# Smaller weight buffers, a fixed order of products: an edit to the GEMM pipeline of a two-layer decoder trunk

## The chip, the cores and the metric

The kernel runs on one core of one Trainium2 chip. The metric is the device time of one execution in microseconds (us), the median of several runs. Each core has five engines with a queue each: TensorE (PE; its weight loader is shown as PEld), VectorE (DVE), ScalarE (ACT), GpSimd (POOL) and SyncE (SP). DMA transfers are issued from the queues of SP and ACT and carried by 16 DMA engines. PE reads weights and activations from on-chip memory (SBUF) and adds up its products in PSUM.

## The reference: what is computed

A decoder trunk of two layers over 272 tokens (16 learned meta tokens and 256 of the sequence), width 2048, 16 heads of 128, in float32. Layer 0 uses attention with forget gates, layer 1 stick-breaking attention over a K/V that is projected once. Each layer ends with a squared-ReLU MLP of inner width 8192. Cut to what matters:

```python
a = rms_norm(h, norm_attn[0])
q, k, v, f_logit = split(a @ fox_w_in[0])            # 2048 -> 3*2048 + 16
o = forgetting_attention(q, k, v, cumsum(log_sigmoid(f_logit + fox_b_f[0])))
h = h + o @ fox_w_o[0]
h = h + squared_relu_mlp(rms_norm(h, norm_mlp[0]), w_up[0], w_down[0])
a, c = rms_norm(h, norm_attn[1]), rms_norm(h, kv_norm)
o = stick_breaking_attention(a @ sb_w_q[0], *split(c @ w_kv))
h = h + o @ sb_w_o[0]
h = h + squared_relu_mlp(rms_norm(h, norm_mlp[1]), w_up[1], w_down[1])
return rms_norm(h, final_norm)[:, 16:]               # without the meta tokens
```

## The kernel before

**Layout.** Everything is feature-major: activations are tiles of 128 features by 272 tokens, 16 such chunks for the width of 2048 (`hT`, the residual stream). In layer 1, where the output needs only the 256 sequence tokens, most products have 256 columns.

**Split numbers.** PE multiplies operands of type F32R. To keep float32 accuracy, each operand is split into a high part, which is the F32R copy made by ACT, and a low part, which is what DVE finds left over. A product of weight and activation is then three products on PE: high x high (line 220), high x low (221) and low x high (222). In layer 1 the groups are "paired" (`pairs`): the high and low activations lie side by side, 512 columns wide, so line 217 multiplies both with the high weights in one product, and line 218 multiplies the high activations with the low weights (256 columns). Splits of the weights are made on the chip as they are read: `whi` (line 197, ACT) and `wlo` (line 198, DVE), two chunks of 512 columns (a half) at a time.

**A GEMM group** (`gemm_group`, line 161) makes 512 output features, in four accumulators of 128 features (`accs`, index `m`), from 2048 input features. It takes its weights in four quarters (`kb`) of four input chunks (`kc`) each. For each quarter it loads 1 MB of weights into one raw buffer (`raw`, pool `wraw`, three buffers, line 185, issued from SP), splits it as two halves (`hf`, pool `wspl`, three buffers each for `whi` and `wlo`), and then writes down the products. The order of the products (lines 203 to 207) is: in quarters 0 to 2, first half before second half, and in each half output chunk by output chunk; in the last quarter output chunk by output chunk through all four input chunks, so that the accumulators are finished one after another. After the last product of an output chunk its evacuation (`evac`) is written down. The very first group (`load_x` set) also loads the activations, in smaller pieces, and runs its first quarter input chunk by input chunk.

There are 96 groups: 12 for q, k and v of layer 0 (four heads each), 4 for its output projection (`out_proj`, line 432), 32 for its MLP (`mlp`, line 444: four passes of four `up` and four `down` groups), 4 for q and 8 for k and v of layer 1, 4 for its output projection, and 32 for its MLP. The 40 groups of q, output projection and MLP in layer 1 are paired.

**Evacuation.** An `up` group reads an accumulator, multiplies with the norm's factor and ReLU (line 457), squares (459) and splits the result (460, 461). In a paired group `total` (line 230) first copies the accumulator's second half out with ACT (234) and adds the first half with DVE (235). Output projections and `down` groups add to `hT` on DVE (line 228). Norm factors come from `Norm.finish` (line 142), which starts with one product on PE (line 145).

**Order of the work.** The program is written as a sequence, and a scheduler with its own timing model decides the order in each engine's queue before the run. An engine works its queue in that order. An instruction waits for what it reads, and for buffers to come free: `whi` waits for the products that read the buffer before, the load of `raw` for the split that read it before, and the first product into an accumulator for that accumulator's evacuation. The scheduler may put products in another order than the program has them. Products of the attention (fp32, among lines 302 to 429 and 504 to 584) are queued between those of the GEMM groups. `tc.issue_after` (line 201) is the one place in `gemm_group` that fixes an order by hand: work in `after` is queued behind the quarter's splits.

Of the kernel before, what the change touches and what calls it, by code (L numbers as in the profile page):

```python
# [9 lines left out]
F32 = mybir.dt.float32  # L10
# [5 lines left out]
P = 128  # L16
# [16 lines left out]
def yoco_kernel(ctx: ExitStack, tc: tile.TileContext, hT_in, gains, b_f, w_f, w_qkv0, w_o0, w_up, w_dn,  # L33
                w_kv, w_q1, w_o1, outT):
    nc = tc.nc

    const = ctx.enter_context(tc.tile_pool(name="const", bufs=1))
    wraw = ctx.enter_context(tc.tile_pool(name="wraw", bufs=3))

    align = ctx.enter_context(tc.tile_pool(name="align", bufs=1))  # L40
    wspl = ctx.enter_context(tc.tile_pool(name="wspl", bufs=3))
    xs = ctx.enter_context(tc.tile_pool(name="xs", bufs=2))
    tmp = ctx.enter_context(tc.tile_pool(name="tmp", bufs=2))
    att = ctx.enter_context(tc.tile_pool(name="att", bufs=2))
# [112 lines left out]
            return r  # L157

    uid = [0]

    def gemm_group(wblk, sp, t0, evac, before={}, after={}, load_x=None, pairs=False, apart=()):

        uid[0] += 1
        u = uid[0]
        accs = [pacc.tile([P, 512], F32, tag="acc", name=f"acc_{u}_{m}") for m in range(4)]
        n = T - t0  # L170
        for kb in range(4):
            raw = wraw.tile([P, 4, 512], F32, tag="raw", name=f"raw_{u}_{kb}")
            src_w = wblk[kb].rearrange("p (k c) -> p k c", k=4)
            if kb in before:
                before[kb]()
            piece = 4 if load_x is None else (1, 2, 2, 4)[kb]
            for k0 in range(0, 4, piece):
                if load_x is not None:
                    load_x(range(4 * kb + k0, 4 * kb + k0 + piece))
                if load_x is not None and kb == k0 == 0:  # L180

                    for c0 in (0, 256):
                        nc.scalar.dma_start(raw[:, 0, c0:c0 + 256], src_w[:, 0, c0:c0 + 256])
                else:
                    nc.sync.dma_start(raw[:, k0:k0 + piece], src_w[:, k0:k0 + piece])
            piece = min(piece, 2)
            parts = []
            for hf in range(2):
                whi = wspl.tile([P, 2, 512], F32R, tag="whi", name=f"whi_{u}_{kb}_{hf}")
                wlo = wspl.tile([P, 2, 512], F32R, tag="wlo", name=f"wlo_{u}_{kb}_{hf}")  # L190
                boxes = [(o, piece, 0, 512) for o in range(0, 2, piece)]
                if load_x is not None and kb == hf == 0:
                    boxes[:1] = [(0, 1, 0, 256), (0, 1, 256, 512)]
                for o, no, c0, c1 in boxes:
                    src = raw[:, 2 * hf + o:2 * hf + o + no, c0:c1]
                    hp, lp = whi[:, o:o + no, c0:c1], wlo[:, o:o + no, c0:c1]
                    on_act = nc.scalar.activation(hp, src, AF.Copy)  # L197
                    on_dve = nc.vector.tensor_tensor(out=lp, in0=src, in1=hp.bitcast(F32), op=ALU.subtract)  # L198
                parts.append((whi, wlo))
            if kb in after:  # L200
                with tc.issue_after(on_act.ins), tc.issue_after(on_dve.ins):
                    after[kb]()
            order = [(kc, m) for hf in range(2) for m in range(4) for kc in range(2 * hf, 2 * hf + 2)]
            if load_x is not None and kb == 0:
                order = [(kc, m) for kc in range(4) for m in range(4)]
            if kb == 3:
                order = [(kc, m) for m in range(4) for kc in range(4)]
            for kc, m in order:
                whi, wlo = parts[kc // 2]
                k = 4 * kb + kc  # L210
                wh = whi[:, kc % 2, m * P:(m + 1) * P]
                wl = wlo[:, kc % 2, m * P:(m + 1) * P]
                first = kb == 0 and kc == 0
                last = kb == 3 and kc == 3
                hi, lo = sp.hi[:, k], sp.lo[:, k]
                if pairs and m not in apart:
                    nc.tensor.matmul(accs[m], wh, sp.both[:, k], start=first, stop=False)  # L217
                    nc.tensor.matmul(accs[m][:, :n], wl, hi, start=False, stop=last)  # L218
                else:
                    nc.tensor.matmul(accs[m][:, :n], wh, hi, start=first, stop=False)  # L220
                    nc.tensor.matmul(accs[m][:, :n], wh, lo, start=False, stop=False)  # L221
                    nc.tensor.matmul(accs[m][:, :n], wl, hi, start=False, stop=last)  # L222
                if last:
                    evac(m, [accs[m][:, :n]] + ([accs[m][:, n:]] if pairs and m not in apart else []))

# [17 lines left out]
    def load_x(chunks):  # L243
        c0, n = chunks[0], len(chunks)
        nc.sync.dma_start(hT[:, c0:c0 + n, :], hT_in[:, c0:c0 + n, :])
        if c0 == 0:
            nc.sync.dma_start(g_sb, gains)
        for c in chunks:
            split_chunk(xa, G_A0, c)
# [79 lines left out]
    for g in range(4):  # L329
# [11 lines left out]
        if g == 0:  # L341
            gemm_group(w_qkv0[0], xa, 0, evac_q, after={kb: (lambda kb=kb: first_norm(kb)) for kb in range(4)}, load_x=load_x)
            forget_gates(box["rstd"])
        else:
            gemm_group(w_qkv0[3 * g], xa, 0, evac_q)
# [4 lines left out]
        def decays(j):  # L350

            for i, (o, n) in enumerate(((0, 144), (144, T))):
                nc.vector.scalar_tensor_tensor(out=s[:, j, o:o + n], in0=fk[:, j, :n],
                                               scalar=fq_sb[:, i, 4 * g + j:4 * g + j + 1],
                                               in1=maskA[:, o:o + n], op0=ALU.subtract, op1=ALU.add)

        gemm_group(w_qkv0[3 * g + 1], xa, 0, lambda m, acc: evac_kv(m, acc, kT),
                   after={j: (lambda j=j: decays(j)) for j in range(4)})

# [263 lines left out]
    for i in range(2):  # L623
        pr = patt.tile([P, 512], F32, tag="patt", name=f"pr_fin_{i}")
        for b in range(2):
            nc.tensor.matmul(pr[:, b * P:(b + 1) * P], rs[:, b:b + 1].to_broadcast([P, P]), ident,
                             start=True, stop=True)
# [67 lines left out]
```

## Time and profile before

| | |
|---|---|
| median of 3 runs | 2360.81 us (2360.66 to 2361.17) |
| the profiled execution | 2360.31 us |
| its span, first to last instruction | 2358.6 us |
| mean granted TensorE clock | 0.998 |
| PE / DVE / ACT busy | 99% / 57% / 45% |
| DMA: mean rate, share of 16 engines (SP's and ACT's queues) | 175 GB/s, 48.9% |
| weight loads of 1 MB: number, median time to landing | 381, 4.8 to 4.9 us |
| one `whi` / one `wlo` of two chunks | 1.05 us / 1.22 us |

How to read the lines that follow in this document: a timeline line has the start in us from the span's start, the duration in us, the engine, the line of the kernel, the operation, out<-in by the program's names, the shape, the count, and in brackets the engine's idle time before it with what ended it. A line of the waits has who waited, for whom, the us in total, how often, and the longest. PE's ends are modelled, because matmuls are pipelined; its starts are not, so spans on PE are best taken from start to start.

### The profile page before, as it was taken

The numbers are of one execution on the slowest core, as the hardware profiler recorded it, in microseconds if no ns is written. First come the engines' busy times: TensorE is split into PE (matmuls) and PEld (weight loads), VectorE is DVE, ScalarE is ACT, GpSimd is POOL, SyncE is SP. The second block draws the span as 40 slices with busy tenths as digits, with TensorE's granted clock in tenths as the row PEclk, the third lists the DMA queues.
The fourth block names the chain that finished last, engine by engine and source line by source line (L and its number), as shares of the span: only waits on it lengthen the run. The fifth ranks groups of instructions, "written<-read, shape, count | busy, mean of one in ns | idle before, by whom it ended". The sixth has DMA issues, their size and how long they took to land.

```text
span 2358.6 us, 39145 instructions
## 1 busy us (share of the span) xinstructions
PE 2344.8 (99%) x16512; PEld 2211.8 (94%) x16512; DVE 1343.1 (57%) x1916; ACT 1057.1 (45%) x1471; POOL 35.9 (2%) x64
## 2 busy tenths in 40 slices
PE   9999999999999999999999999999999999999998
PEld 9999999999999999999998999988888888888887
DVE  7565555655455455445566555566555655655665
ACT  5443344543344344344445444445543543543543
POOL 0000000000000000000000000000000000000000
PEclk9999999999999999999999999999999999999999
DMA  6444444554545455554545444445555555455453
GB/s 235 145 164 171 155 159 163 176 180 169 189 163 186 171 180 178 179 179 173 178 168 197 156 147 145 144 177 180 183 178 193 192 183 197 169 190 195 178 196 125
DMA packets 61039, 411.92 MB, mean 175 GB/s; under 512 B 7088, under 2 KB 10048, under 8 KB 12096
## 3 DMA queue, kind: packets, MB, share of 16 engines
q1 hardware_dynamic: 58976, 406.27, 48.5%
q8 instruction: 129, 2.11, 0.4%
q10 hardware_dynamic: 1888, 3.16, 0.4%
q14 instruction: 46, 0.38, 0.0%
HBM read 407.29 MB, written 2.11 MB: 174 GB/s over the span
## 4 chain that ended last, share of the span: by engine, by line
PE 99%; DVE 0%; ACT 0%; DMA 0%; issue 0%; DVEq 0%; SPq 0%; ACTq 0%
PE acc L217 25%; PE acc L220 19%; PE acc L221 19%; PE acc L222 19%; PE acc L218 13%; PE ps L365 0%; PE pza L542 0%; PE pv L307 0%; PE po L426 0%; PE po L427 0%; PE po L581 0%; PE po L582 0%; PE pzb L543 0%; PE po L428 0%; DMA g_sb<-gains 0%; ACT whi L197 0%
## 5 line engine op out<-in xcount | busy, mean ns | idle before, releaser
L198 DVE TENSOR_TENSOR wlo<-raw,whi 128x1024 fp32r<-128x1024 f32 (+1 forms) x771 | 932.5, 1220 | 761.5 <-ACT whi L197 758.2
L197 ACT ACTIVATE whi<-raw 128x1024 fp32r<-128x1024 f32 (+1 forms) x771 | 803.2, 1054 | 1072.4 <-PE acc L221 678.3
L217 PE MATMUL acc<-x_m,whi 128*128 128x512 f32 x1024 | 343.1, 394 | 0.5 <-DVE relu L235 0.5
L217 PE MATMUL acc<-x_u,whi 128*128 128x512 f32 x1008 | 337.9, 394 | 0.0
L220 PE MATMUL acc<-x_u,whi 128*128 128x272 f32 (+1 forms) x1040 | 297.7, 289 | 0.0
L221 PE MATMUL acc<-x_u,whi 128*128 128x272 f32 (+1 forms) x1040 | 294.8, 286 | 0.0
L220 PE MATMUL acc<-x_m,whi 128*128 128x272 f32 x1024 | 293.4, 289 | 0.0
L221 PE MATMUL acc<-x_m,whi 128*128 128x272 f32 x1024 | 290.4, 286 | 0.0
L222 PE MATMUL acc<-x_u,wlo 128*128 128x272 f32 (+1 forms) x1040 | 285.2, 284 | 0.0
L222 PE MATMUL acc<-x_m,wlo 128*128 128x272 f32 x1024 | 280.7, 284 | 0.0
L218 PE MATMUL acc<-x_m,wlo 128*128 128x256 f32 x1024 | 252.6, 282 | 0.0
L218 PE MATMUL acc<-x_u,wlo 128*128 128x256 f32 x1008 | 247.6, 281 | 0.0
L220 PE MATMUL acc<-x_a,whi 128*128 128x272 f32 x768 | 222.1, 294 | 0.7 <-ACT x_a L122 0.7
L221 PE MATMUL acc<-x_a,whi 128*128 128x272 f32 x768 | 221.0, 292 | 0.0
L217 PEld LDWEIGHTS acc<-x_m,whi 128*128 128x128 f32 x1024 | 185.0, 188 | 30.3 <-DVE relu L235 0.9
L222 PE MATMUL acc<-x_a,wlo 128*128 128x272 f32 x768 | 210.5, 287 | 0.0
L218 PEld LDWEIGHTS acc<-x_m,wlo 128*128 128x128 f32 x1024 | 192.3, 188 | 19.4 <-DVE wlo L198 4.6
L217 PEld LDWEIGHTS acc<-x_u,whi 128*128 128x128 f32 x1008 | 182.4, 188 | 29.7
L218 PEld LDWEIGHTS acc<-x_u,wlo 128*128 128x128 f32 x1008 | 189.3, 188 | 15.9 <-DVE wlo L198 1.6
L220 PEld LDWEIGHTS acc<-x_u,whi 128*128 128x128 f32 x1040 | 195.5, 188 | 0.2
L221 PEld LDWEIGHTS acc<-x_u,whi 128*128 128x128 f32 x1040 | 195.3, 188 | 0.1
L220 PEld LDWEIGHTS acc<-x_m,whi 128*128 128x128 f32 x1024 | 192.5, 188 | 0.0
(246 smaller groups left out, 3613.0 us busy)
## 6 DMA issues: line engine op xcount, KB each, us to landing
raw<-w_up SPq DMA_DIRECT2D x128, 1024.0 KB, 4.9
raw<-w_dn SPq DMA_DIRECT2D x128, 1024.0 KB, 4.9
raw<-w_qkv SPq DMA_DIRECT2D x45, 1024.0 KB, 4.8
raw<-w_o SPq DMA_DIRECT2D x32, 1024.0 KB, 4.8
raw<-w_kv SPq DMA_DIRECT2D x32, 1024.0 KB, 4.9
raw<-w_q SPq DMA_DIRECT2D x16, 1024.0 KB, 4.8
fk<-f_dram ACTq DMA_DIRECT2D x4, 544.0 KB, 5.2
raw<-w_qkv SPq DMA_DIRECT2D x4, 512.0 KB, 8.3
```

What stands on the lines that cost most here:

```text
L197: on_act = nc.scalar.activation(hp, src, AF.Copy)
L198: on_dve = nc.vector.tensor_tensor(out=lp, in0=src, in1=hp.bitcast(F32), op=ALU.subtract)
L217: nc.tensor.matmul(accs[m], wh, sp.both[:, k], start=first, stop=False)
L218: nc.tensor.matmul(accs[m][:, :n], wl, hi, start=False, stop=last)
L220: nc.tensor.matmul(accs[m][:, :n], wh, hi, start=first, stop=False)
L221: nc.tensor.matmul(accs[m][:, :n], wh, lo, start=False, stop=False)
L222: nc.tensor.matmul(accs[m][:, :n], wl, hi, start=False, stop=last)
```

## The change

There are four parts.

1. A quarter's raw weights go into two tiles of two chunks (`raws`), with four buffers in the pool, in place of one tile of four chunks with three buffers. Each half is loaded by its own DMA of 512 KB. In the first group the pieces of the last quarter are two chunks as well.
2. The pool of split weights has four buffers for each of `whi` and `wlo` in place of three. Together the two pools take the same memory as before: 24 + 24 KB per partition before, 16 + 32 KB after.
3. The first quarter of a group is ordered like the last: output chunk by output chunk through all four input chunks. The first group keeps its own order there.
4. All products of a group go through `gemm_matmul`, which ties each to the one before it, across groups too, with an edge that the scheduler must keep but that makes no wait on the chip. In the first group the edges are left out.

```diff
-    wraw = ctx.enter_context(tc.tile_pool(name="wraw", bufs=3))
+    wraw = ctx.enter_context(tc.tile_pool(name="wraw", bufs=4))
-    wspl = ctx.enter_context(tc.tile_pool(name="wspl", bufs=3))
+    wspl = ctx.enter_context(tc.tile_pool(name="wspl", bufs=4))
...
+    queued, pinned = [], [False]
+
+    def gemm_matmul(*args, **kw):
+
+        ins = nc.tensor.matmul(*args, **kw).ins
+        if queued and pinned[0]:
+            tc.add_manual_dep(ins, queued[0].name, mybir.DependencyInfo(mybir.DependencyClass.NoSync,
+                                                                        mybir.DependencyReason.DATA))
+        queued[:] = [ins]
...
-            raw = wraw.tile([P, 4, 512], F32, tag="raw", name=f"raw_{u}_{kb}")
...
-            piece = 4 if load_x is None else (1, 2, 2, 4)[kb]
+            piece = 1 if load_x is not None and kb == 0 else 2
+            raws = [wraw.tile([P, 2, 512], F32, tag="raw", name=f"raw_{u}_{kb}_{hf}") for hf in range(2)]
...
-                    nc.sync.dma_start(raw[:, k0:k0 + piece], src_w[:, k0:k0 + piece])
-            piece = min(piece, 2)
+                    nc.sync.dma_start(raws[k0 // 2][:, k0 % 2:k0 % 2 + piece], src_w[:, k0:k0 + piece])
...
-                    src = raw[:, 2 * hf + o:2 * hf + o + no, c0:c1]
+                    src = raws[hf][:, o:o + no, c0:c1]
...
             if load_x is not None and kb == 0:
                 order = [(kc, m) for kc in range(4) for m in range(4)]
-            if kb == 3:
+            elif kb in (0, 3):
                 order = [(kc, m) for m in range(4) for kc in range(4)]
+            pinned[0] = load_x is None
...
-                    nc.tensor.matmul(accs[m], wh, sp.both[:, k], start=first, stop=False)
-                    nc.tensor.matmul(accs[m][:, :n], wl, hi, start=False, stop=last)
+                    gemm_matmul(accs[m], wh, sp.both[:, k], start=first, stop=False)
+                    gemm_matmul(accs[m][:, :n], wl, hi, start=False, stop=last)
```

The three products of an unpaired group (lines 220 to 222) are changed to `gemm_matmul` in the same way.

More of the change, by code (lines that the diff above doesn't have):

```diff
@@ L182, in gemm_group @@
                     for c0 in (0, 256):
-                        nc.scalar.dma_start(raw[:, 0, c0:c0 + 256], src_w[:, 0, c0:c0 + 256])
+                        nc.scalar.dma_start(raws[0][:, 0, c0:c0 + 256], src_w[:, 0, c0:c0 + 256])
                 else:
-                    nc.sync.dma_start(raw[:, k0:k0 + piece], src_w[:, k0:k0 + piece])
-            piece = min(piece, 2)
+                    nc.sync.dma_start(raws[k0 // 2][:, k0 % 2:k0 % 2 + piece], src_w[:, k0:k0 + piece])
             parts = []
@@ L216, in gemm_group @@
                 if pairs and m not in apart:
-                    nc.tensor.matmul(accs[m], wh, sp.both[:, k], start=first, stop=False)
-                    nc.tensor.matmul(accs[m][:, :n], wl, hi, start=False, stop=last)
-                else:
-                    nc.tensor.matmul(accs[m][:, :n], wh, hi, start=first, stop=False)
-                    nc.tensor.matmul(accs[m][:, :n], wh, lo, start=False, stop=False)
-                    nc.tensor.matmul(accs[m][:, :n], wl, hi, start=False, stop=last)
+                    gemm_matmul(accs[m], wh, sp.both[:, k], start=first, stop=False)
+                    gemm_matmul(accs[m][:, :n], wl, hi, start=False, stop=last)
+                else:
+                    gemm_matmul(accs[m][:, :n], wh, hi, start=first, stop=False)
+                    gemm_matmul(accs[m][:, :n], wh, lo, start=False, stop=False)
+                    gemm_matmul(accs[m][:, :n], wl, hi, start=False, stop=last)
                 if last:
```

## The prediction

> **What bounds the kernel now.** I read the page's busy shares first, then the chain that ended last, then the waits, then the timelines of a few group boundaries.
>
> ```profile
> span 2358.6 us, 39145 instructions
> ...
> PE 2344.8 (99%) x16512; PEld 2211.8 (94%) x16512; DVE 1343.1 (57%) x1916; ACT 1057.1 (45%) x1471; POOL 35.9 (2%) x64
> ...
> PE 99%; DVE 0%; ACT 0%; DMA 0%; issue 0%; DVEq 0%; SPq 0%; ACTq 0%
> ```
>
> TensorE (PE) sets the end: the chain that ended last is PE for 99%. Ends of matmuls are modelled, so I went by starts. In the PE timeline a 272-column product starts 124.4 ns after the one before it on average, a 512-column one keeps PE 232 ns and a 256-column one 118 ns. A group of layer 0 (192 products) thus takes 23.89 us from its first product to the next group's first, and 30 of the 32 MLP groups there read exactly that (the others 23.90 and, with the norm's product inside, 24.11). A paired group of layer 1 (64 x (232 + 118) ns) takes 22.43 us. Whatever is above these two lengths is all that an edit of order and buffers can win.
>
> The 40 paired groups take 903.5 us together; 40 x 22.43 = 897.2, so 6.3 us are above. The waits of the weight loader say where:
>
> ```profile
> PEld acc L218 <- DVE wlo L198: 7.0, 18, 0.4
> ...
> PEld acc L217 <- DVE qT L235: 1.3, 1, 1.3
> PEld pms_a L145 <- DVE ssq_a L140: 1.2, 1, 1.2
> ...
> PEld acc L217 <- DVE relu L235: 0.9, 1, 0.9
> ```
>
> Eighteen times a low-part product (L218) waits for its split (`wlo`); twice a group's first product waits for the evacuation of the group before; once the norm's product waits. One of the eighteen, in the second `up` group of a pass:
>
> ```profile
> 1857.14 1.08 PE L217 MATMUL acc<-x_m,whi 128*128 128x512 f32 x4
> 1858.17 0.39 PE L218 MATMUL acc<-x_m,wlo 128*128 128x256 f32 x1
> ```
>
> Four L217 in a row: the scheduler queued high-part products ahead because it held the low part to be late, and it is. The last of the four starts at 1857.83 and the L218 at 1858.17, 340 ns where 232 is usual. The reason stands on ScalarE (ACT) and VectorE (DVE) around the boundary at 1848.7:
>
> ```profile
> 1846.92 0.83 ACT L234 COPY relu<-acc 128x256 f32<-128x256 f32 x2 [2.66 <-PE acc L218]
> 1848.08 1.06 ACT L197 ACTIVATE whi<-raw 128x1024 fp32r<-128x1024 f32 x1 [0.33 <-PE acc L217]
> ...
> 1849.35 1.05 ACT L197 ACTIVATE whi<-raw 128x1024 fp32r<-128x1024 f32 x1
> ...
> 1851.48 0.35 ACT L234 COPY relu<-acc 128x256 f32<-128x256 f32 x1
> ...
> 1855.80 2.96 ACT L197 ACTIVATE whi<-raw 128x1024 fp32r<-128x1024 f32 x3 [0.73 <-PE acc L217]
> ```
>
> ```profile
> 1849.17 2.48 DVE L198 TENSOR_TENSOR wlo<-raw,whi 128x1024 fp32r<-128x1024 f32 x2 [0.30 <-ACT whi L197]
> ...
> 1852.57 0.42 DVE L235 TENSOR_TENSOR relu<-acc,relu 128x256 f32<-128x256 f32 x1
> ```
>
> The last quarter holds two of the three split buffers, so the next group's second half is split only at the boundary (1848.08), amid the evacuations; accumulator 3 is free at 1852.99 (1852.57 + 0.42), 4.3 us after the boundary; the first quarter's products are shuffled around it, hold their buffer longer, and the split at 1855.80, then its `wlo` at 1856.89 + 1.22 = 1858.1, comes late.
>
> **The change part by part.**
>
> *Four split buffers.* The last quarter holds two, so the next group's first quarter finds two others, released when the third quarter's halves end: 8.4 and 5.6 us before the boundary. A split is 1.05 us (`whi`) + 1.22 us (`wlo`), so both halves can be done 3 us before the boundary. The next splits take the last quarter's buffers, 0.7 us before and at the boundary, and are due 5.6 and 8.4 us after it. The eighteen waits lose their cause. I count the groups one by one: of the 6.3 us, 0.4 belong to the norm's product in two groups, 0.3 to attention products in the first output projection, 0.1 to the last group with its chunk apart; these stay. The rest, **5.4 us**, goes: some 0.19 in each of 18 groups (3.4), 0.2 of small pieces, and 1.1 and 0.7 at the two boundaries that wait for an evacuation, where the copies of two or three finished accumulators are queued on ACT behind a `whi` that sits 2.46 us for its buffer.
>
> *First quarter chunk by chunk.* The second half is now due 2 x 0.35 = 0.70 us after the boundary (layer 0: 6 x 0.1244 = 0.75) instead of 2.8 (3.0); accumulator 3 is due 12 x 0.35 = 4.2 us after it (layer 0: 4.5) instead of 2.1. Against the 4.3 us at which it is free today that lacks 0.1 us; if nothing moved, the 16 `up` and 4 `q` groups would lose 20 x 0.1 = 2 us. But the copies of chunks 0 to 2 no longer share those microseconds with a blocked `whi`, so between 0 and 2 I take **0.5 us** lost. The order itself costs nothing: in layer 0 quarters in either order take 5.97 us.
>
> *Queued as written.* Nothing overtakes in the products' queue: a late split or accumulator holds all products behind it, where today others go first. The cover is the lead above; its absence is the second rival. Attention products stay free.
>
> *Half-size raw buffers.* 388 loads on SP become 769; 381 more issues of 0.33 to 0.43 us are some 150 us of SP, which waits 1950.8 us today:
>
> ```profile
> SPq L185 <- DVE wlo L198: 1950.8, 348, 13.2
> ```
>
> A packet of 8192 bytes (309 ns in the trace's packet records) becomes two of 4096 (159 each): 9 ns x 48768 / 16 engines = 27 us more per DMA engine, 48.5% to some 49.7% of the span; hidden. Raw data ahead falls from 12 chunks to 8, 4 halves of 2.8 to 3.0 us each, some 11 us. A 512 KB load is not in the steady trace: between a 256 KB store (3.0 us) and the 1 MB load (4.9); I take 3.6. Eleven covers it: 0, and the third rival if not.
>
> *Start.* The norm's product waits from 31.05 + 0.12 to 32.28, because ACT squares the last chunks behind `whi` that wait for a buffer (0.77 and 0.55 us) and because the last activations come as one load behind 1 MB transfers (ACT waits 0.78). Both ease; between 0 and 1.1 I take **0.6 us** won.
>
> *Switches.* 107 changes from products to attention matmuls and 107 back take 17.2 + 7.8 us from start to start, 0.117 each on average, while single ones reach 0.21 to 0.33. Some ten more or fewer dear ones (0.2 over the average) are 2 us either way; I take 0.
>
> Sum: -5.4 + 0.5 - 0.6 = **-5.5 us**. The profiled execution took 2360.31 us (span 2358.6 and 1.7 around it), which becomes 2354.8; the median of the runs is 0.5 higher, so **2355.3 us**, 0.23% less.
>
> A rule speaks against the halves. The rows first: from 10 to 25 us the DMA engines were busy throughout and moved 409 GB/s, with four loads of 512 KB among them; the kernel's mean is 175. The Trainium skill (DMA: Bandwidth & Descriptors, "Measured" and "Rules for kernel authors") wants at least 1 MiB per DMA for three quarters of peak bandwidth. By that rule the loads would run further below peak, and the sum would change only once they set the end; with several in flight the trace disagrees, and one at a time is the third rival.
>
> **The rivals.**
>
> 1. *The waits only change place* (2360, 0.20). The boundary work is the same: 8 splits and four evacuations per group, ACT busy 12.0 and DVE 13.9 us of 22.6 in an `up` group. If the in-order queues put a blocked `whi` ahead of the copies as before, the fixed order turns 0.18 us of shuffling into 0.1 to 0.3 us of waiting: 2360.8 less the start's 0.6. For it: ACT's copies do wait behind such a `whi` now. Against: the fourth buffer takes the block away from the copies of chunks 0 to 2. It also covers the case that the pinned queue changes nothing that matters.
>
> 2. *The second half comes late in attention stages* (slower, 0.14). At the end of a K group DVE is full (5.75 of 6 us from 147 to 153), and the two splits there end at 147.6 and 149.3, with the boundary at 147.0. Were the second still at 149.3, 2.3 us after, the fixed order would wait 2.3 - 0.75 = 1.5 us; in the 20 groups next to attention 30 us: 2355.3 + 30 = 2385. It decides as soon as that split ends over 0.75 us after the boundary. Against: its buffer is free 5.6 us ahead, when DVE is half idle (3.6 of 7 us from 140 to 147).
>
> 3. *Loads become the bound* (0.03). One at a time a half takes 3.6 + 0.4 us of issue against 2.9 of use: 768 x 1.1 = 845 us more, 3200. Against: four in flight, 11 us of lead.
>
> 4. *The spacing of products itself shrinks* (0.03). Rows: 124.4 ns for 272 columns, 232 for 512, 118 for 256, whatever the order. If order set the spacing, even 1% of 2239 us would be 22 us: 2333. The Trainium skill (TensorE: Matmul & The Clock Gate, "Back-to-back issue gap") gives columns / 2.4 + 2.5 ns, by an estimate from that page 116 ns for 272 columns, so by that rule there is room. The trace shows equal quarters in both orders, so I give it little.
>
> **How the numbers follow.** Forecast case 0.60 (own range 2353 to 2357.5), rivals 0.20, 0.14, 0.03, 0.03. A measurement of this kernel tells about 0.2% from no change: below 2356.1 is faster. Of the forecast case 0.48 lies below that, 0.12 above. Faster 0.48 + 0.03 = 0.51; same 0.12 + 0.20 = 0.32; slower 0.14 + 0.03 = 0.17. Low end: 5.4 + 1.1 + 2 = 8.5 won and nothing lost, 2352.3, and 0.4 for the spread of the runs: 2351.9. High end: the first rival and 2 us of switches, with the same spread: 2362.5. Outside lie rivals 2 to 4, 0.20.
>
> **What would show it.** L217 and L218 alternate strictly in layer 1; the L218 waits for `wlo` fall from 7.0 us to under 1; the L217 waits for `qT` and `relu` are gone; all paired groups but four read 22.43 us. Wrong: PE waiting at 0.7 or 4.2 us after boundaries (for `wlo`, or an evacuation), `whi` waiting for a raw load, attention groups longer than now.

## The result, and the profile after

The changed kernel takes **2366.08 us** in the median of 22 runs, against 2360.78 us for 22 runs of the kernel before beside it: 5.3 us more (0.22%), where 5.5 less was forecast. The runs fall into two groups: seventeen lie at 2365.4 to 2367.1, five at 2354.9 to 2357.4, and nothing lies between. The ratio over all of them, 1.0015 (95% interval 1.0009 to 1.0020), is a mean of the two. The profiled execution (2366.38 us) belongs to the upper group.

Its page, with the span, the busy times, SP's DMA queue and the chain's shares:

```profile
span 2364.7 us, 40002 instructions
...
PE 2349.5 (99%) x16512; PEld 2218.4 (94%) x16512; DVE 1342.9 (57%) x1916; ACT 1061.4 (45%) x1471; POOL 36.6 (2%) x64
...
q1 hardware_dynamic: 113984, 406.29, 52.1%
...
PE 99%; DVE 0%; DMA 0%; ACT 0%; issue 0%; DVEq 0%; ACTq 0%
```

PE still sets the end. Its count of instructions is the same and its busy time is 4.7 us longer. So this is no new bound; the same products take longer. The waits of the weight loader in the changed kernel:

```profile
PEld pms_a L145 <- DVE ssq_a L140: 3.6, 1, 3.6
...
PEld acc L164 <- DVE relu L244: 0.6, 1, 0.6
```

The eighteen waits for `wlo` (7.0 us before) and the waits at group boundaries for `qT` and `relu` are gone, as forecast (one new wait for a `relu` stands in their place, 0.6 us). The wait of the first norm's product (L145) has grown from 1.2 to 3.6 us. Three points in each trace show where the time is: the first product of the second group, the first of layer 1's first q group, and the end. The last column adds up the 40 paired groups, each from its first product to the first of the next group, without the time of products that do not belong to a group.

| profiled execution | span | second group starts | from there to layer 1 | layer 1 to the end | the 40 paired groups |
|---|---|---|---|---|---|
| before | 2358.6 | 38.8 | 1167.7 | 1152.1 | 903.5 |
| changed, upper group | 2364.7 | 44.4 | 1167.6 | 1152.7 | 904.7 |
| changed, lower group (first experiment) | 2355.1 | 43.3 | 1167.6 | 1144.2 | 896.2 |

The middle of the program, with all of layer 0's loads and attention, is unchanged to 0.1 us. The start costs 4.4 to 5.6 us. Layer 1 is either 7.9 us shorter, or 0.6 longer. These are two separate questions.

**The start.** ACT in the changed kernel, while PE finishes the first group (its last product starts at 31.36):

```profile
29.31 1.06 ACT L205 ACTIVATE whi<-raw 128x1024 fp32r<-128x1024 f32 x1 [1.77 <-PE acc L164]
30.27 0.41 ACT L139 ACTIVATE sq_a<-hT 128x272 f32<-128x272 f32 x1
31.77 1.06 ACT L205 ACTIVATE whi<-raw 128x1024 fp32r<-128x1024 f32 x1 [1.08 <-DMA raw<-w_qkv]
32.73 0.41 ACT L139 ACTIVATE sq_a<-hT 128x272 f32<-128x272 f32 x1
```

The same part of ACT's queue in the kernel before:

```profile
29.00 1.06 ACT L197 ACTIVATE whi<-raw 128x1024 fp32r<-128x1024 f32 x1 [0.77 <-PE acc L221]
29.97 0.74 ACT L139 ACTIVATE sq_a<-hT 128x272 f32<-128x272 f32 x2
31.25 1.06 ACT L197 ACTIVATE whi<-raw 128x1024 fp32r<-128x1024 f32 x1 [0.55 <-PE acc L221]
```

And PE in the changed kernel after it:

```profile
31.36 0.28 PE L164 MATMUL acc<-x_a,wlo 128*128 128x272 f32 x1
35.03 1.27 PE L145 MATMUL pms_a<-ssq_a,mean_w 128*128 128x272 f32 x2 [3.39 <-DVE ssq_a L140]
...
36.79 0.43 PE L287 MATMUL pf<-x_a,wf_hi 128*16 128x272 f32 x1
37.01 0.43 PE L288 MATMUL pf<-x_a,wf_hi 128*16 128x272 f32 x1
```

The last two squares of the norm (L139) stand in ACT's queue each behind a `whi` of the second group; 15 splits are queued ahead of the last square, 13 in the kernel before. The new buffers allowed the scheduler to put these splits so early. (The fourth split buffer and the half-size raw buffers come together in every run here, so which of the two it takes is not shown.) One split then waits 1.77 us for a buffer that the first group's last products hold, the other 1.08 us for its load. PE starts nothing for 3.67 us, and the products behind the gap start 227 ns apart (36.79 to 37.01 and on) where 125 is usual. The windows from 35 to 40 us say why: the granted clock (the number behind the five busy times) is half.

```profile
35.00:40.00 5.00, 4.97 (x20) 3.12 (x21) 2.56 (x7) 0.86 (x2) 0.00 (x0) 0.50 0.41 156
```

In the kernel before, where the gap was 1.2 us, it is 1.00:

```profile
35.00:40.00 5.00, 5.00 (x43) 4.10 (x41) 3.77 (x10) 0.12 (x1) 0.24 (x1) 1.00 0.11 44
```

Narrower windows of the changed kernel's trace read 1.00 up to 34.4 us, 0.50 from there to 41.2, and 1.00 again behind it; in the lower trace the half is granted from 35.1 to 38.5 only, and its start costs 1.1 us less. The Trainium skill (TensorE: Matmul & The Clock Gate, "HAM oscillation — how this bites in real kernels") warns of idle gaps over some 3.4 us, after which the array runs at half clock; the trace agrees in the main: 3.67 us from start to start went with a clock of 0.50, 1.2 us with 1.00, though the clock fell at 34.4 us already, 3.0 us after the last start.

**Layer 1.** In the changed kernel the products alternate strictly, one of 512 columns (`whi`), one of 256 (`wlo`). The same stretch of PE in the upper and in the lower group of runs, each from one high product to the eighth after it:

```profile
2249.76 0.40 PE L164 MATMUL acc<-x_m,whi 128*128 128x512 f32 x1
2250.00 0.28 PE L164 MATMUL acc<-x_m,wlo 128*128 128x256 f32 x1
...
2252.60 0.39 PE L164 MATMUL acc<-x_m,whi 128*128 128x512 f32 x1
```

```profile
2249.89 0.40 PE L164 MATMUL acc<-x_m,whi 128*128 128x512 f32 x1
2250.13 0.28 PE L164 MATMUL acc<-x_m,wlo 128*128 128x256 f32 x1
...
2252.69 0.39 PE L164 MATMUL acc<-x_u,whi 128*128 128x512 f32 x1
```

Eight pairs take 2.84 us in the one and 2.80 in the other, with no wait in either. The start-to-start times repeat every three pairs: 231, 118, 233, 123, 237, 118 ns (1060 together) or 229, 120, 229, 118, 232, 119 (some 1046). A group of 64 pairs takes **22.61 us** in the first pattern and **22.33** in the second, and each pattern lasts to the end of the kernel. In layer 1 both runs go alike until one product in the second `up` group of layer 1's MLP, which waits for accumulator 3; in the upper group

```profile
1653.96 0.51 PE L164 MATMUL acc<-x_m,whi 128*128 128x512 f32 x1 [0.25 <-DVE relu L244]
```

and the same product in the lower group

```profile
1652.85 0.50 PE L164 MATMUL acc<-x_m,whi 128*128 128x512 f32 x1 [0.25 <-DVE relu L244]
```

After it the upper run reads 22.61 in the groups that follow, the lower one 22.33. With some 30 groups left, 30 x 0.28 = 8.4 us is most of the 9.6 us between the two traces; 1.1 us of the rest is the start. The 22.43 that I took for the length of a paired group was no length that a fixed order keeps; in the kernel before it is what a shuffled order comes to.

### The profile page after: what moved, and what is told of

It reads as the page before. It is cut to its first block, busy times and chain, and to the rows that moved or that the text cites. A ratio compares the mean times of both kernels' runs of the same rounds, so it can differ in the third digit from the quotient of the medians.

```text
span 2364.7 us, 40002 instructions
## 1 busy us (share of the span) xinstructions
PE 2349.5 (99%) x16512; PEld 2218.4 (94%) x16512; DVE 1342.9 (57%) x1916; ACT 1061.4 (45%) x1471; POOL 36.6 (2%) x64
## 3 DMA queue, kind: packets, MB, share of 16 engines
q1 hardware_dynamic: 113984, 406.29, 52.1%
## 4 chain that ended last, share of the span: by engine, by line
PE 99%; DVE 0%; DMA 0%; ACT 0%; issue 0%; DVEq 0%; ACTq 0%
PE acc L164 95%; PE ps L374 0%; DMA raw<-w_qkv 0%; PE pza L551 0%; PE pv L316 0%; PE po L435 0%; PE po L436 0%; PE po L590 0%; PE po L591 0%; PE pzb L552 0%; PE po L437 0%; DVE wlo L206 0%; PE pf L287 0%; PE pf L288 0%; PE pf L289 0%; PE po L592 0%
## 5 line engine op out<-in xcount | busy, mean ns | idle before, releaser
L164 PE MATMUL acc<-x_m,whi 128*128 128x272 f32 (+1 forms) x3072 | 744.9, 324 | 0.2 <-DVE relu L244 0.2
L164 PE MATMUL acc<-x_u,whi 128*128 128x272 f32 (+2 forms) x3088 | 744.8, 323 | 0.0
L164 PE MATMUL acc<-x_u,wlo 128*128 128x272 f32 (+1 forms) x2048 | 579.5, 283 | 0.0
L164 PE MATMUL acc<-x_m,wlo 128*128 128x272 f32 (+1 forms) x2048 | 579.5, 283 | 0.0
L164 PE MATMUL acc<-x_a,whi 128*128 128x272 f32 (+1 forms) x1792 | 386.6, 308 | 0.5 <-ACT x_a L122 0.5
L164 PEld LDWEIGHTS acc<-x_m,wlo 128*128 128x128 f32 x2048 | 384.6, 188 | 0.0
L164 PEld LDWEIGHTS acc<-x_u,wlo 128*128 128x128 f32 x2048 | 384.6, 188 | 0.0
L164 PEld LDWEIGHTS acc<-x_a,whi 128*128 128x128 f32 x1792 | 288.0, 189 | 13.6 <-ACT x_a L122 0.8
L164 PE MATMUL acc<-x_a,wlo 128*128 128x272 f32 (+1 forms) x1024 | 288.0, 285 | 0.0
L164 PE MATMUL acc<-x_kv,whi 128*128 128x272 f32 x1024 | 195.8, 289 | 0.0
```

The costliest lines, as they stand in the source:

```text
L164: ins = nc.tensor.matmul(*args, **kw).ins
```

## Experiments

Two theories came out of this. **The start** (C in the expectations): the norm's squares stand behind splits that the new buffers let in early, and the long gap halves the clock. Its rival, D, was that the new loads come late. **Layer 1** (A): strict alternation has two spacings, and the last disturbance before a stretch of it picks one. The other letters are rivals or variants of these, with their numbers in each expectation. Each of the three batches has its own runs of the kernel before, at 2360.4 to 2360.7 us.

| profiled execution | span | second group starts | from there to layer 1 | layer 1 to the end | paired groups |
|---|---|---|---|---|---|
| no edges | 2358.7 | 43.7 | 1167.6 | 1147.5 | 899.6 |
| edges alone | 2394.5 | 39.2 | 1167.5 | 1187.8 | 938.4 |
| buffers alone | 2358.8 | 43.0 | 1167.5 | 1148.2 | 899.6 |
| squares first | 2359.2 | 38.5 | 1167.6 | 1153.2 | 904.7 |
| and norm earlier | 2358.3 | 38.0 | 1167.6 | 1152.7 | 904.2 |
| and extra products | 2355.8 | 37.9 | 1167.6 | 1150.4 | 901.8 |
| squares first, two and two | 2339.5 | 37.8 | 1167.6 | 1134.1 | 885.6 |
| and norm earlier | 2337.9 | 38.0 | 1167.6 | 1132.4 | 884.3 |
| and unpaired by two chunks | 2343.8 | 37.8 | 1172.5 | 1133.5 | 884.3 |
| before, two and two | 2340.2 | 38.6 | 1167.7 | 1134.0 | 885.4 |
| four and four | 2339.0 | 38.0 | 1167.6 | 1133.4 | 885.6 |

### The changed kernel again

No edit.

> The changed kernel, unchanged. Its 22 runs fell into two groups, 2355 to 2357.4 and 2365.4 to 2367.1 us. Theory A (spacing): the strictly alternating 512- and 256-column products of layer 1 settle into one of two regular spacings, 1046 or 1060 ns per three pairs, and the last disturbance decides which; then every undisturbed paired group of this trace reads either 22.33 or 22.61 us, and a trace from the low group of runs has most of the 40 at 22.33. Rival B (start): the two groups differ only at the start, by whether the granted clock drops in the wait for the norm's product; then paired groups read 22.61 whatever the time, and the second group's first product starts at 38 to 40 us in a low run and at 44.4 in a high one.

2357.65 us in the median of 12 runs, ratio 0.9998 (0.9987 to 1.0009). The two groups are there again, with other shares: nine runs at 2355.6 to 2358.8, three at 2366.1 to 2368.3. Its profiled execution is the lower trace shown above: from the wait on its groups read 22.33, as A has it, so B (the runs differ at the start alone) is out. The same program on another chip thus comes out 3 us below the kernel before or 5 above it; a median of this kernel says mostly which group has more runs.

### The four parts taken apart

Without the edges (`e2_no_pin`):

```diff
-            pinned[0] = load_x is None
+            pinned[0] = False
```

> The changed kernel without the edges between products: buffers, half-size loads and the order of the first quarter stay, the scheduler may shuffle products again. Theory A: groups in which it shuffles change spacing inside, and paired groups read mixed values between 22.3 and 22.6 (mean 22.45 to 22.5); the time is 2360 to 2363 and less spread. Rival E (memory): the long spacing of layer 1 comes from the 512 KB loads or from where the four split buffers lie, not from the order; then the paired groups stay at 22.61 and the time at 2366. Start as in the changed kernel under both (the second group from about 44 us).

2360.86 us (10 runs within 2360.0 to 2361.5), ratio 1.0002 (0.9993 to 1.0011): one group. The scheduler shuffles again, the paired groups read 22.4 to 22.6, and the late start remains (43.7).

The edges alone, in the kernel before (`e3_pin_alone`):

```diff
-                    nc.tensor.matmul(accs[m], wh, sp.both[:, k], start=first, stop=False)
+                    gemm_matmul(accs[m], wh, sp.both[:, k], start=first, stop=False)
...
```

> The kernel before with the edges alone: 1 MB loads, three buffers, old order of the first quarter, but products queued as written. Theory A: undisturbed stretches of paired products read 22.33 or 22.61 per group, as in the changed kernel, although loads and buffers are the old ones. Rival E: they read 22.43 as before. Under both, what the old buffers cost without shuffling shows on top: waits for the low-part split and for accumulators at group boundaries in layer 1, 0.1 to 1 us per group, time 2358 to 2390 us. The start is that of the kernel before (second group from about 38.8 us).

2397.22 us, ratio 1.0157 (1.0144 to 1.0170). The order as written, with the old buffers and the old first quarter, waits in twenty groups for the evacuation of the group before:

```profile
PEld acc L164 <- DVE relu L245: 25.6, 16, 1.6
...
PEld acc L164 <- DVE qT L245: 6.4, 4, 2.1
```

The second group starts at 39.2, near the 38.8 of before. So the edges by themselves bring these waits, and the other parts of the change take them away (which part, was not separated); the edges have no part in the late start. Between the waits the products run at the two spacings of A: from 1750 us on, for one, at 1060 ns per three pairs, and two late groups read 22.33.

The buffers and half loads alone, with the old first quarter and no edges (`e4_buffers_alone`):

```diff
-            elif kb in (0, 3):
+            if kb == 3:
...
-            pinned[0] = load_x is None
+            pinned[0] = False
```

> The kernel before with the new buffers alone (four split buffers, raw weights in four halves, 512 KB loads); old order of the first quarter, no edges. The start should be that of the changed kernel if the fourth split buffer lets two splits in ahead of the last squares: norm's wait about 3.4 us, second group from about 44 us, +5.5. In layer 1 the scheduler still shuffles, so paired groups read mixed values; with the eighteen waits for low parts gone, a mean of 22.40 to 22.45. Time 2359 to 2363 us in one group of runs. If loads of 512 KB or their buffers cost anything in the steady part, layer 0's groups would read above 23.89.

2360.36 us, ratio 1.0000 (0.9991 to 1.0009). Within it two effects cancel: the start is 4.2 us later (43.0 against 38.8), layer 1 is 3.9 us shorter (1148.2 against 1152.1). The late start belongs to the buffers and half loads.

### The start: squares ahead of the splits

In the changed kernel the last square and its sum must stand ahead of the first of the second group's splits; the edge fixes an order in the queue and makes no wait:

```diff
+            if self.label == "a0":
+                squared[:] = [on_act.ins, on_dve.ins]
...
+                    if u == 2 and kb == hf == 0:
+                        for ins, done in zip((on_act.ins, on_dve.ins), squared):
+                            tc.add_manual_dep(ins, done.name, ...NoSync...)
```

> The changed kernel, with the squares of the first norm queued ahead of the second group's weight splits on ACT and DVE (an edge that makes no wait). Theory C (queue order at the start): the norm's product waits 3.4 us because the last two squares stand on ACT behind two splits that the fourth buffer let in; then the wait is gone (under 0.3 us), the granted clock stays at 1.0, the second group's first product starts at 38 to 39 us instead of 44.4, and both groups of run times move down by 5 to 7 us (to about 2360 and 2350.5). Rival D (loads): the start is late because only 8 chunks of raw weights are ahead instead of 12; then the wait stays at 2 us or more. If theory B holds, the runs no longer fall into two groups; if A holds, they still do.

2356.43 us, ratio 0.9982 (0.9972 to 0.9993); six runs at 2351.2 to 2352.5 and six at 2360.4 to 2361.0. PE goes from the first group to the norm without a gap, and the window from 35 to 40 us has the full clock, with loads still moving at 270 GB/s:

```profile
31.91 0.29 PE L167 MATMUL acc<-x_a,wlo 128*128 128x272 f32 x1
32.03 0.62 PE L147 MATMUL pms_a<-ssq_a,mean_w 128*128 128x272 f32 x2
```

```profile
35.00:40.00 5.00, 5.00 (x43) 4.18 (x41) 4.20 (x11) 0.45 (x2) 0.24 (x1) 1.00 0.83 270
```

The second group starts at 38.5: 5.9 us won, all of the loss at the start. The rival of late loads falls as a cause by itself: ACT still waits for a load here, 0.35 us at 32.5 us, but nothing of the norm stands behind it. Both groups of runs moved down and the distance of 9 us stayed, so the start is not what splits the runs.

### The wait that picks: the norm's product one quarter earlier

On top of it, the norm's product of the first `up` and the first q group is written before the third quarter, not the fourth. With the edges it had moved from 9.4 us into its group to 17, so the evacuations of that group, which need the norm, came late, and accumulator 3 with them.

```diff
-            gemm_group(w_up[layer, f, g], xm, t0, evac, {3: get_rstd} if f == g == 0 else {},
+            gemm_group(w_up[layer, f, g], xm, t0, evac, {2: get_rstd} if f == g == 0 else {},
-        gemm_group(w_q1[g], xq, M, evac_q1, {3: get_rstd1} if g == 0 else {},
+        gemm_group(w_q1[g], xq, M, evac_q1, {2: get_rstd1} if g == 0 else {},
```

> Squares first as in the run before it, and the norm's product asked for one quarter earlier (before the third quarter instead of the last) in the first q group and the first up groups. Theory A: in the second up group of layer 1 PE waits some 0.4 us for the last accumulator of the group before, whose evacuations pile up because the norm's product comes only 17.2 us into its group; a jitter of 10 ns in the end of that wait chooses the spacing of the 30 groups behind it. With the product at about 11 us the pile and the wait go, nothing chooses by chance, and the runs form one group: 2350 to 2352 us if the spacing after the norm's product stays the short one (as in the three traces so far), 2358 to 2360 if not. Rival F: the choice is not tied to that wait; then two groups of runs 9 us apart remain.

2359.99 us, ratio 0.9997 (0.9988 to 1.0006); eleven runs within 2358.9 to 2360.8. The wait is gone and so is the second group of runs: that wait did the picking. (Why it comes out one way in one run and the other way in the next is not shown; the two traces differ by 0.01 us in it.) But now the norm's product itself is the last disturbance, and it leads into the long spacing: the groups of the trace read 22.61, and the times of all eleven runs go with that.

### Extra products as disturbances

On top of the kernel above, one more small product (32, 64, 96 and 128 columns, into a spare bank; its result is not used) ahead of the `down` groups of each of layer 1's four MLP passes:

```diff
+            if layer == 1:
+                kick = patt.tile([P, 512], F32, tag="patt", name=f"kick_{f}")
+                gemm_matmul(kick[:, :32 * f + 32], nones_r, ntri_r[:, :32 * f + 32], ...)
```

> As the run with the earlier norm product, and one extra product (32, 64, 96 and 128 columns, F32R, its result is not used) in front of the first down group of each of the four passes of the last MLP. Theory A: each extra product can move the stream from one spacing to the other; between two of them all groups read the same value, 22.33 or 22.61, and at least one of the four changes it, for 8 groups (2.2 us) at a time, though the products themselves take 0.2 us together. Rival H: only a wait can change the spacing (or a place in memory sets it); then all 32 groups read what they read without the extra products.

2358.08 us, ratio 0.9991 (0.9982 to 1.0000). From start to start the groups read 22.61 after the first and second extra product, **22.33** in the eight groups from the third (96 columns) to the fourth, and 22.61 again after the fourth (128). One small product changes the length of every group behind it by 0.28 us, both ways. This is the most direct evidence for A.

### Another order: two high, two low

In the kernel with the squares first, paired products are written high, high, low, low over two input chunks:

```diff
                     gemm_matmul(accs[m], wh, sp.both[:, k], start=first, stop=False)
-                    gemm_matmul(accs[m][:, :n], wl, hi, start=False, stop=last)
+                    held.append((wl, hi, last))
+                    if len(held) == 2:
+                        for wl, hi, end in held:
+                            gemm_matmul(accs[m][:, :n], wl, hi, start=False, stop=end)
+                        held = []
```

> Squares first, and in paired groups the products of two input chunks are written high, high, low, low (512, 512, 256, 256 columns) in place of high, low, high, low. Same products, same columns. Theory A (order sets the spacing): another regular pattern; stretches of that kind in the trace of before read some 347.5 ns per pair, so a group 22.2 to 22.4 us, and no second value 0.28 us above; time 2349 to 2352 in one group of runs. Rival G (columns alone set the spacing, and what differs between runs is something else): groups read 22.33 or 22.61 as with strict alternation, runs at 2351.5 and 2360.5.

**2341.28 us**, ratio 0.9918 (0.9905 to 0.9932), four runs within 0.7 us, and far below the 2349 to 2352 expected. Nearly every paired group reads 22.08 us, where 22.2 to 22.4 were expected. The stretch of PE that was shown above:

```profile
2249.88 0.62 PE L167 MATMUL acc<-x_u,whi 128*128 128x512 f32 x2
2250.33 0.40 PE L167 MATMUL acc<-x_u,wlo 128*128 128x256 f32 x2
...
2252.64 0.62 PE L167 MATMUL acc<-x_u,whi 128*128 128x512 f32 x2
```

Eight pairs take 2.76 us, against 2.80 and 2.84 in strict alternation. The disturbances (the same wait in the second `up` group, 1.3 us here) no longer matter for what comes after.

### All three together, and its neighbours

With the norm one quarter earlier as well (`e9_best`):

> The changed kernel with the last squares of the first norm queued ahead of the second group's splits, the norm's product one quarter earlier in its group, and the paired products written two high, two low. If the spacing is set by the order of the products and held, every paired group reads 22.1 us, the wait of 1.3 us for the accumulator in the second group of each layer-1 MLP pass is gone from its first pass, and the time is 2339.5 to 2340.5 us with all runs within 1 us of each other. If the norm's earlier product disturbs this order as it did the strict alternation, some of the paired groups go back above 22.3 and the time is 2345 us or more.

**2340.02 us**, ratio 0.9915 (0.9902 to 0.9929), runs from 2339.6 to 2341.6 (2 us apart, where 1 was expected): the wait of 1.3 us is gone, and every group but those with a norm's product, attention or the last chunk apart reads 22.08. This is the fastest of all kernels here.

The same idea for the unpaired groups, whose products all have 272 columns (`e10_triples`): by two chunks, each of the three kinds twice in a row.

```diff
+                        for wh, wl, hi, lo, start, end in held:
+                            gemm_matmul(accs[m][:, :n], wh, hi, start=start, stop=False)
+                        for wh, wl, hi, lo, start, end in held:
+                            gemm_matmul(accs[m][:, :n], wh, lo, start=False, stop=False)
+                        for wh, wl, hi, lo, start, end in held:
+                            gemm_matmul(accs[m][:, :n], wl, hi, start=False, stop=end)
```

> The kernel above, and the unpaired products (three of 272 columns for each chunk) written by two chunks: high-high twice, high-low twice, low-high twice, outside the first group. If the order matters only where products of two widths alternate, the 112 unpaired groups stay at 23.89 us and the time is that of the kernel above within 1 us. If changing weights with the same moving tile in a row counts by itself, as the 126 to 127 ns products of the first group of the kernel before suggest, these groups go to about 24.1 and the time rises by some 10 us or more.

2345.82 us, ratio 0.9937 (0.9924 to 0.9951): 5.8 us more than the kernel above on the same chip. The undisturbed unpaired groups read 24.00 us instead of 23.89; of the two expectations the second has the sign, with half its size. (The expectation speaks of 112 unpaired groups; there are 56.) So order counts with products of one width too, and there the order as it was is the better one.

The order alone, in the kernel before, with its three buffers, 1 MB loads and no edges (`e11_before_two_and_two`):

```diff
-                    nc.tensor.matmul(accs[m][:, :n], wl, hi, start=False, stop=last)
+                    held.append((wl, hi, last))
+                    if len(held) == 2:
+                        for wl, hi, end in held:
+                            nc.tensor.matmul(accs[m][:, :n], wl, hi, start=False, stop=end)
+                        held = []
```

> The kernel before with nothing changed but the order in which the paired products are written: two high, two low. If the order of the products is what the time of layer 1 hangs on, its groups go from 22.43 us on average towards 22.1 without the new buffers and without the edges, and the time is 2345 to 2355 us. If the saving needs the edges, because the scheduler orders products by when their tiles are ready whatever was written, the groups stay at 22.4 and the time at 2359 to 2362 us.

**2341.93 us**, ratio 0.9921 (0.9907 to 0.9934). It is more than the 2345 to 2355 expected, and nothing of the change is needed for the gain. The scheduler still shuffles, but it does so by the new pieces:

```profile
1907.12 0.62 PE L218 MATMUL acc<-x_u,whi 128*128 128x512 f32 x2
1907.58 0.40 PE L222 MATMUL acc<-x_u,wlo 128*128 128x256 f32 x2
1907.82 1.54 PE L218 MATMUL acc<-x_u,whi 128*128 128x512 f32 x6
1909.19 0.87 PE L222 MATMUL acc<-x_u,wlo 128*128 128x256 f32 x6
1909.89 2.00 PE L218 MATMUL acc<-x_u,whi 128*128 128x512 f32 x8
```

Nearly all products come in rows of two, four, six or eight of a kind, and the groups read 22.0 to 22.15 us. What differs is how many high products stand alone between two low ones: from 1550 us on these are 1523 of the kernel before's 2238 high ones, and 19 of 2228 here. This count goes with the gain, but the neighbours alone do not fix the time of a product: from 1550 us on, a high product with high ones on both sides takes 231.9 ns on average in the kernel before and 229.2 here. The eighteen waits of low products for `wlo` are gone as well, without a fourth buffer: written later, these products are due later.

Rows of four in the first and last quarter (`e12_four_and_four`):

```diff
-                    if len(held) == 2:
+                    if len(held) == (4 if kb in (0, 3) else 2):
```

> The first of these kernels with four high and four low products in turn in the first and last quarter of each paired group, two and two in the middle quarters. If the gain is that fewer changes between the two widths are paid, each quarter of four and four is shorter by what half of its changes cost and the time falls below that of two and two, by 2 to 6 us. If the period is a matter of how the two widths fit and not of the number of changes, the groups can be longer: 22.2 to 22.4 us and 2345 us or more.

2340.84 us, ratio 0.9917 (0.9903 to 0.9930): groups of 22.11 to 22.15, against 22.08. Longer rows win nothing more, so the saving does not grow with fewer changes of width; in every kernel here in which hardly a paired product stands alone, the undisturbed paired groups read 22.01 to 22.15 us.

## Why the prediction was wrong

Two terms of the sum failed, by about 6 us each in the profiled execution: the paired groups were to come to 903.5 - 5.4 + 0.5 = 898.6 us and came to 904.7, and the start was to win 0.6 us and lost 5.6. The lower group of runs (2354.9 to 2357.4 us) comes near the forecast of 2355.3 by luck: its start lost 4.4 us, and its layer 1 won 7.9 where 4.9 was forecast.

- **"The order itself costs nothing" is the step that failed in layer 1.** It rested on layer 0, where quarters in both orders read 5.97 us; there all products have one width. For the paired groups I took 22.43 us as their length "whatever is above". The runs show 22.61 or 22.33 for strict alternation, 22.08 for two and two, and a mixture of about 22.4 to 22.6 for shuffled ones. At the long spacing a group costs 0.18 us more than I reckoned, and most of the 40 groups of the upper trace ran at it, which takes back all that the waits were worth (6.3 at most).
- **The start** is the other step that failed. I looked at what the halves and the fourth buffer ease on ACT, and not at what the scheduler would queue in the room they give: two more splits, ahead of the norm's last squares. Some 2.45 us of the loss is the longer gap, and some 3.1 us is half of the 6.2 us (35.0 to 41.2) in which the products behind it ran at half clock. Squares first took away all of it.
- **The split buffers** did what was said. The eighteen waits and the two boundary waits are gone; the buffers alone shorten the paired groups by 3.9 us (903.5 to 899.6), of 5.4 forecast, and the lower group of runs, with a spacing 0.10 below my 22.43, saves 7.3 in these groups.
- **The accumulator's 0.5 us** was forecast in the sum for 20 groups at up to 0.1 each. It came at one place: the low product ahead of it was followed after 526 ns, where 118 is usual, and it took 343 ns itself, where 231 is usual: 0.5 us in all. That it would decide the next 700 us was not foreseen.
- **Loads and switches at 0** hold: from the second group to layer 1 the time is 1167.5 to 1167.7 us with either size of load, and the half loads land in 3.8 to 4.3 us (3.6 was taken). SP's queue took 52.1% of the DMA engines' time, not 49.7, and that was hidden too. The third rival is out, and so is the second: the attention of layer 0 lies within that stretch, and the stretch from layer 1's first group to the second `up` group, with its attention, went from 439.3 to 437.4 us. The Trainium skill (DMA: Bandwidth & Descriptors, "Rules for kernel authors") asks for at least 1 MiB per DMA where bandwidth is to be highest; with up to four loads of 512 KB in flight the traces show no loss of time at 174 GB/s. The prediction's window from 10 to 25 us is a weak test, since three loads of 1 MB were issued in it as well; but the changed kernel, with no load over 512 KB there, moved 396 and 408 GB/s from 10 to 15 and 15 to 20 us, against 402 and 421 before.
- **The first rival** (waits only change place) has nearly the time of the upper group without its start, 2360.4 to 2361.0, and not its mechanism: but for one wait of 0.6 us, none took the place of those removed.
- **The fourth rival**, order sets the spacing, was the mechanism, and I gave it 0.03. It named a gain alone; the order of this change lengthens the spacing in the upper group of runs. The argument against it ("equal quarters in both orders") came from the unpaired groups alone, and I never sorted the paired products by what stands before and behind them.

What stays open is why PE has these spacings at all, and why one run of a program falls into the one and the next into the other. That the spacings depend on order, last as long as nothing disturbs them, and can be switched by one product is shown; which part of PE or its weight loads makes the period of three pairs is not. The Trainium skill (TensorE: Matmul & The Clock Gate, "Back-to-back issue gap") gives columns / 2.4 + 2.5 ns for a matmul by itself, by an estimate from that page 325 ns for a pair; no order here came below 344.

## What to carry to other kernels

Where PE is 99% busy, the spacing of its products is the first thing to question, and its start-to-start times in every stage are the view to take it from: an average over a shuffled order is not a floor. Try other orders of products of two widths: rows of two of each in place of single ones were worth 19 us of 2360 here, more than all waits together, while for products of one width two of a kind in a row cost 5.8. A buffer more is also room for the scheduler: look at what it will queue early in that room, and ahead of what.

## What the runs showed of the hardware

- Two streams of the same alternating products ran at 1046 or 1060 ns per three pairs for hundreds of microseconds, with no wait and a granted clock of 1.00, and one extra product of 96 or 128 columns moved them from one to the other.
- With rows of two, the period is 1380 ns for four pairs (229, 232, 113, 114, 226, 229, 120, 117), 345 for a pair; a 256-column product took 113 to 120 ns, a 512-column one 226 to 232.
- Products of 272 columns took 124.4 ns on average in the order high-high, high-low, low-high (127, 125, 121 in turn), and 125.0 with each kind twice.
- After a gap of 3.7 to 4.0 us from product to product the mean clock from 35 to 40 us was 0.50 to 0.66 (four traces), so that the gap cost more than itself; through gaps of 1.2 us (kernel before) and up to 2.0 us (edges alone, 1279 to 1283 us) it stayed 1.00.
